# Column sums of squares: a group of four products waits for all four squares

## The chip, the cores and the metric

One Trainium2 chip, one of its cores. The metric is the time of one execution on the device in microseconds; lower is better. Names of engines: PE is TensorE's matmul, PEld its weight load, DVE is VectorE, ACT is ScalarE, POOL is GpSimd, SP is SyncE.

## The reference

A two-layer decoder trunk in float32. 512 prompt tokens and 8 x 4 sample tokens, 544 columns in all, of 1024 channels. Layer 0 mixes tokens by causal pooling, layer 1 by a gated linear recurrence (HGRN2); each is followed by a gated ConvFFN. Every sub-layer has a norm ahead of it and one behind it:

```python
def rmsnorm(x, g):
    xf = x.astype(jnp.float32)
    r = lax.rsqrt(jnp.mean(xf * xf, axis=-1, keepdims=True) + EPS)
    return (xf * r * g.astype(jnp.float32)).astype(x.dtype)

for li in range(DEPTH):
    h = rmsnorm(x, norm_mix_pre[li])
    m = pool_mixer(h, ...) if li % 2 == 0 else hgrn_mixer(h, ...)
    x = x + rmsnorm(m, norm_mix_post[li])
    h = rmsnorm(x, norm_ffn_pre[li])
    m = conv_ffn(h, ...)          # gelu(conv(h @ w_up)) * ..., then @ w_down
    x = x + rmsnorm(m, norm_ffn_post[li])
```

What matters here is the mean of x*x over the 1024 channels, for every token.

## The kernel before

Channels lie on the 128 partitions in eight tiles (k = 0 to 7), tokens along the free dimension, cut into a first half of 256 columns and a second of 288 (256 prompt tokens and the 32 samples). The large products of the layers, which I call ordinary matmuls, run with each operand split into a high and a low part and three matmuls per tile (xh or oh and xl or k are the split activations, wh and wl the split weights; of the names in the lists below, ps and pa are PSUM banks).

A norm's sum over channels is a sum over partitions and over the eight tiles. ScalarE squares each tile (sqs[k], a tile named t). The function colsums then multiplies each square with a 128x32 block of ones (from the tile cs), in full float32 precision, so that 32 partitions of the result hold the sum of that tile. Tile k goes to the partitions 32*(k % 4) to 32*(k % 4) + 31 of one bank named pr; tiles 4 to 7 are added on top of 0 to 3. Four products of one call therefore write four different strips of 32 partitions and use four different strips of 32 columns of the matmul array. Behind them, ScalarE copies the bank out (t<-pr), col_rstd sums the four strips by three small products (pr<-cs,t, 128x1 and 32x1), VectorE works out the reciprocal root in a chain of small operations (tiles named c) and scales a unit matrix by it, and one product with ones (pr<-t,cs 128x256 or 128x288) spreads the factor over all partitions, from where ScalarE copies it to R. Results of a large product leave PSUM by a VectorE multiplication with R.

colsums is called twice (tiles 0 to 3, then 4 to 7) for each half at four norms: in project (the pooled layer's output) and in Residual.start_b (the norm ahead of a ConvFFN or of HGRN2, when the sub-layer before it is added to x). That makes 64 products, 32 of 256 columns and 32 of 288.

The order of the instructions is not that of the code. Every operation is recorded by Plan; Plan.emit is a list scheduler with a cost and a latency per engine, which writes out the order of all five engines. It takes at each step the operation that can start first by its estimates, and of those that can start at the same time one of a pr bank first, then the one with the longest tail behind it. Plan.after(a, b, ...) adds to the next recorded operation a dependency on the last writer of each tile given. In colsums each product has its own square as an input, and Plan.after adds the square of the last tile of the call. ScalarE's squares are scheduled as well, so the square of the last tile is not always the last to be made.

Of the kernel before, what the change touches and what calls it, by code (L numbers as in the profile page):

```python
# [345 lines left out]
def trunk_step(ctx: ExitStack, tc: _tile.TileContext, xT, xp, xs, spool, s0, fctx, par, gb0, cst, bands,  # L346
               pw, wup, wdn, win, wout, yT, yB, o_pp, o_ps, o_hp, o_hs, o_ff):
    nc = tc.nc
    plan = Plan(tc)
# [300 lines left out]
    def colsums(pn, sqs, ks):  # L650

        for k in ks:
            j = k % 4 * 32
            plan.after(sqs[ks[-1]])
            PE.matmul(pn[j:j + 32], ones[:, 0:32], sqs[k], start=(k < 4), stop=(k >= 4), skip_group_check=True)

    def spread(dg, out):
# [74 lines left out]
    class Residual:  # L732
# [10 lines left out]
        def start_b(self, hf):  # L743
# [17 lines left out]
            for k0, k1 in (((0, 2), (2, 4), (4, 6), (6, 8)) if gnext is None else ((0, 1), (1, 2), (2, 4), (4, 6), (6, 8))):  # L761
                mk = m[:, k0:k1, sl]
                if self.gpost is None:
                    DVE.tensor_tensor(mk, mk, rpost.unsqueeze(1).broadcast_to([P, k1 - k0, n]), op=ALU.mult)
                else:
                    for k in range(k0, k1):
                        DVE.scalar_tensor_tensor(m[:, k, sl], m[:, k, sl], pcol(self.gpost + k), rpost, op0=ALU.mult, op1=ALU.mult)
                if gnext is None:

                    POOL.dma_start(yT[:, k0:k1, sl], mk, accum_op=ALU.add)  # L770
                    continue
                xs_ = xs_of(k0, k1, sl)
                DVE.tensor_tensor(xs_, xs_, mk, op=ALU.add)
                for k in range(k0, k1):
                    xk = x_of(k, sl)
                    ACT.activation(oh[:, k, sl], xk, AF.Identity, scale=pcol(gnext + k))
                    sqs[k] = tt((P, n))
                    ACT.activation(sqs[k], xk, AF.Square)
                    if k:
                        low(k - 1)  # L780
                    if k % 4 == 3:
                        colsums(pn, sqs, range(k - 3, k + 1))
# [75 lines left out]
    def project(hf):  # L858
        sl = HV[hf]
        n = sl.stop - sl.start  # L860
        pn = pap.tile([P, 512], F32, tag="pa", name="pr")[:, 0:n]
        sqs = {}
        order = (0, 1, 4, 5, 2, 3, 6, 7)
        for at, o in enumerate(order):
            gi, oc = o // 2, o % 2
            d = ps1()[:, 0:n]
            for kk in range(2):
                s = slice(kk * 256 + oc * P, kk * 256 + (oc + 1) * P)
                PE.matmul(d, pws[gi][:, s], pooled(2 * gi + kk, sl), start=(kk == 0), stop=(kk == 1))
            sq = sqs[at] = tt((P, n))  # L870

            if o % 2:
                DVE.tensor_scalar(mp[:, o, sl], d, pcol(O_PSC + o), None, op0=ALU.mult)
                ACT.activation(sq, mp[:, o, sl], AF.Square)
            else:
                ACT.activation(sq, d, AF.Square, scale=pcol(O_PSC + o))
                ACT.activation(mp[:, o, sl], d, AF.Identity, scale=pcol(O_PSC + o))
            if at % 4 == 3:
                colsums(pn, sqs, range(at - 3, at + 1))
        accp[hf] = tt((P, n))  # L880
        ACT.activation(accp[hf], pn, AF.Identity)
# [910 lines left out]
```

## Time and profile before

| | us |
|---|---|
| median of three runs | 1161.19 |
| lowest and highest | 1158.9, 1162.99 |
| the profiled execution | 1161.18 |
| its span from first to last instruction | 1159.3 |
| TensorE busy in it | 1143.8 |
| VectorE, ScalarE, GpSimd busy | 870.1, 685.8, 406.4 |
| mean granted TensorE clock | 0.995 of full speed |

How to read it: a row of the profile names the line of the code, the engine, the operation, the tile written and the tiles read, the shape and a count; the lines of all recorded operations are that of the scheduler's call (L312), so that tile names tell them apart. A product of float32 stands as two matmul records in the profile and as one row in the lists of instructions here. The halves' column counts, 256 and 288, tell the two halves apart.

### The profile page before, as it was taken

The page shows a single profiled execution, that of the slowest core. Times are in us where ns is not written, and L with a number is a line of the kernel's source. Part 1 is how long each engine was busy: PE and PEld are TensorE (multiplying, and loading weights), DVE is VectorE, ACT ScalarE, POOL GpSimd, SP SyncE. Part 2 cuts the span into 40 slices and gives each one's busy share as a digit, 9 for nine tenths or more (in the row PEclk, how much of TensorE's full clock was granted, in tenths as well). Part 3 has the DMA queues.
Part 4 walks back from the last instruction along what each step waited for, and adds up shares of the span by engine and source line. Part 5 has one row for each costly group of instructions (what it writes and reads, how often), then busy time and mean ns, then how long its engine had stood idle before and what let it go on. Part 6 is the DMA issues. An engine that isn't in the chain of part 4 may idle for free.

```text
span 1159.3 us, 26118 instructions
## 1 busy us (share of the span) xinstructions
PE 1143.8 (99%) x9860; PEld 1104.2 (95%) x9860; DVE 870.1 (75%) x2068; ACT 685.8 (59%) x1459; POOL 406.4 (35%) x729
## 2 busy tenths in 40 slices
PE   8999999999999999999999999999999999999996
PEld 7789999999999998999999999979999999999996
DVE  6679977988788776576766785458986897878865
ACT  4546555656566575566666764455565665656653
POOL 3435222433443332443443420224621434343322
PEclk9999999999999999999999999999999999999999
DMA  9876167676876765777667642573536767777543
GB/s 317 206 189 133 55 175 178 169 179 171 195 172 159 206 208 115 156 149 162 154 157 154 135 127 101 149 188 79 132 83 187 190 167 180 174 169 192 115 127 77
DMA packets 90397, 183.48 MB, mean 158 GB/s; under 512 B 10522, under 2 KB 17050, under 8 KB 90264
## 3 DMA queue, kind: packets, MB, share of 16 engines
q0 software_dynamic: 48272, 91.90, 40.0%
q1 hardware_dynamic: 41856, 89.88, 23.7%
q8 instruction: 77, 1.26, 0.4%
q14 instruction: 48, 0.39, 0.1%
q10 hardware_dynamic: 144, 0.05, 0.0%
HBM read 156.00 MB, written 12.77 MB: 146 GB/s over the span
## 4 chain that ended last, share of the span: by engine, by line
PE 96%; DMA 1%; DVE 1%; ACT 1%; issue 0%; SPq 0%; POOL 0%; DVEq 0%; ACTq 0%; POOLq 0%
PE pa L312 47%; PE ps L312 46%; PE pr L312 3%; DMA t<-bands 1%; DMA wh<-win 0%; DVE t L312 0%; ACT A L312 0%; DVE x L312 0%; ACT t L312 0%; DVE m L312 0%; SPq L312 0%; DVE c L312 0%; ACT wl L312 0%; POOL t L312 0%; DVEq L1772 0%
## 5 line engine op out<-in xcount | busy, mean ns | idle before, releaser
L312 ACT ACTIVATE wh<-raw 128x512 fp32r<-128x512 f32 (+2 forms) x280 | 163.9, 598 | 158.5 <-PE pa L312 59.7
L312 PE MATMUL pa<-op,wh 128*128 128x272 f32 x1152 | 255.7, 288 | 0.0
L312 PE MATMUL ps<-t,wh 128*128 128x272 f32 x1248 | 236.5, 288 | 0.0
L312 DVE TENSOR_TENSOR wl<-raw,wh 128x512 fp32r<-128x512 f32 (+2 forms) x280 | 179.1, 652 | 75.3 <-ACT wh L312 73.2
L312 PE MATMUL pa<-op,wl 128*128 128x272 f32 x768 | 221.2, 288 | 0.0
L312 PEld LDWEIGHTS ps<-t,wh 128*128 128x128 f32 x1248 | 195.9, 188 | 0.0
L312 PEld LDWEIGHTS pa<-op,wh 128*128 128x128 f32 x1152 | 192.9, 188 | 0.0
L312 PE MATMUL ps<-t,wl 128*128 128x272 f32 x624 | 179.5, 288 | 0.0
L312 POOL COPY fst<-t 128x16 f32<-128x16 f32 (+1 forms) x176 | 92.8, 581 | 246.3 <-DVE t L312 246.2
L312 DVE TENSOR_TENSOR t<-t 128x512 f32<-128x512 f32 (+10 forms) x331 | 138.5, 441 | 45.6 <-ACT t L312 23.7
L312 PE MATMUL ps<-xh,wh 128*128 128x256 f32 (+1 forms) x560 | 165.7, 297 | 0.0
L312 PE MATMUL ps<-xl,wh 128*128 128x256 f32 (+1 forms) x560 | 162.3, 290 | 0.0
L312 PE MATMUL ps<-xh,wl 128*128 128x256 f32 (+1 forms) x560 | 161.1, 288 | 0.0
L312 DVE SCALAR_TENSOR_TENSOR t<-t,prm 128x560 f32<-128x560 f32 (+1 forms) x184 | 141.1, 796 | 4.6 <-ACT t L312 3.6
L312 PEld LDWEIGHTS pa<-op,wl 128*128 128x128 f32 x768 | 144.4, 188 | 0.0
L312 PE MATMUL pa<-k,wh 128*128 128x272 f32 (+2 forms) x560 | 137.4, 289 | 0.0
L312 PEld LDWEIGHTS ps<-t,wl 128*128 128x128 f32 x624 | 117.5, 188 | 0.0
L312 ACT ACTIVATE t<-t 128x544 fp32r<-128x544 f32 (+5 forms) x145 | 85.0, 596 | 44.0 <-DVE t L312 42.3
L312 PEld LDWEIGHTS ps<-xh,wh 128*128 128x128 f32 x560 | 105.2, 188 | 3.8 <-issue 0.9
L312 PEld LDWEIGHTS ps<-xl,wh 128*128 128x128 f32 x560 | 105.5, 188 | 2.6 <-issue 2.0
L312 PEld LDWEIGHTS ps<-xh,wl 128*128 128x128 f32 x560 | 105.4, 188 | 2.5 <-issue 2.4
L312 PEld LDWEIGHTS pa<-k,wh 128*128 128x128 f32 x560 | 97.5, 188 | 1.3 <-issue 1.3
(208 smaller groups left out, 2501.9 us busy)
## 6 DMA issues: line engine op xcount, KB each, us to landing
raw<-wup SPq DMA_DIRECT2D x37, 512.0 KB, 3.2
raw<-wup SPq DMA_DIRECT2D x64, 256.0 KB, 3.8
raw<-wup POOLq DMA_DIRECT2D x64, 256.0 KB, 5.8
wh<-win POOLq DMA_DIRECT2D x58, 256.0 KB, 3.4
wl<-win POOLq DMA_DIRECT2D x58, 256.0 KB, 4.7
m<-t POOLq DMA_DIRECT2D x48, 272.0 KB, 6.2
wh<-wup POOLq DMA_DIRECT2D x34, 256.0 KB, 4.2
wl<-wup POOLq DMA_DIRECT2D x34, 256.0 KB, 5.9
```

Source lines behind the costliest of these rows:

```text
L312: o[1](*o[3], **o[4])
```

## The change

In colsums each of the products now depends on the last writers of all the tiles of the call, not on that of the last tile alone:

```diff
         for k in ks:
             j = k % 4 * 32
-            plan.after(sqs[ks[-1]])
+
+            plan.after(*(sqs[q] for q in ks))
             PE.matmul(pn[j:j + 32], ones[:, 0:32], sqs[k], start=(k < 4), stop=(k >= 4), skip_group_check=True)
```

No product, square or copy is added or removed. The scheduler, given the other dependencies, writes out another order. The SP queue's order stays the same; the other four differ in places. Of the sixteen groups of four, six stood together before and do after: four in project, and the two of the first half behind the first ConvFFN, which stand in one row of eight; ten were apart and now stand together.

C, the second half behind the first ConvFFN. PE before (pr_1121 is the bank of the sums, t_1122 to t_1125 are the squares of tiles 0 to 3):

```order
L312 MATMUL ps_1103<-xh_1058,wh_1080 128x256
L312 MATMUL pr_1121<-t_1125,cs_80 32x288
L312 MATMUL ps_1103<-xl_107,wh_1080 128x256
L312 MATMUL ps_1103<-xh_1058,wl_1081 128x256
L312 MATMUL pr_1121<-t_1124,cs_80 32x288
L312 MATMUL ps_1103<-xh_1058,wh_1086 128x256
L312 MATMUL ps_1103<-xl_107,wh_1086 128x256
L312 MATMUL pr_1121<-t_1122,cs_80 32x288
L312 MATMUL ps_1103<-xh_1058,wl_1087 128x256
L312 MATMUL pr_1121<-t_1123,cs_80 32x288
L312 MATMUL ps_1102<-xh_1058,k_1040 128x256
```

Now, at the same place of PE:

```order
L312 MATMUL ps_1102<-xh_1058,k_1044 128x256
L312 MATMUL pr_1121<-t_1122,cs_80 32x288
L312 MATMUL pr_1121<-t_1123,cs_80 32x288
L312 MATMUL pr_1121<-t_1124,cs_80 32x288
L312 MATMUL pr_1121<-t_1125,cs_80 32x288
L312 MATMUL ps_1102<-xl_107,k_1044 128x256
```

The four products have moved together, and the first of them stands nine ordinary matmuls later than the first did. ACT before at C, which makes these squares and those of tiles 4 to 7:

```order
L312 ACTIVATE t_1125<-x_1011 128x288
L312 ACTIVATE t_1124<-x_1011 128x288
L312 ACTIVATE t_1122<-x_1010 128x288
L312 ACTIVATE t_1123<-x_1010 128x288
L312 ACTIVATE xh_1058<-x_1010,prm_79 128x288
L312 ACTIVATE t_1126<-x_1012 128x288
L312 ACTIVATE t_1129<-x_1013 128x288
```

The square of the last tile, t_1125, is the first to be made, and that is the one which each product waited for beside its own. ACT now at the same place:

```order
L312 ACTIVATE t_1124<-x_1011 128x288
L312 ACTIVATE t_1125<-x_1011 128x288
L312 ACTIVATE t_1122<-x_1010 128x288
L312 ACTIVATE t_1123<-x_1010 128x288
L312 ACTIVATE xh_1058<-x_1010,prm_79 128x288
L312 ACTIVATE t_1126<-x_1012 128x288
L312 ACTIVATE t_1127<-x_1012 128x288
```

Four squares ahead of the group, as before, in nearly the same order.

B, the second half of the pooling layer's norm. PE before (pr_250 is the bank, t_251 to t_254 the squares):

```order
L312 MATMUL pr_250<-t_254,cs_80 32x288
L312 MATMUL pa_268<-xh_104,k_200 128x256
L312 MATMUL pa_268<-xl_107,k_200 128x256
L312 MATMUL pr_250<-t_253,cs_80 32x288
L312 MATMUL pa_268<-xh_104,k_202 128x256
L312 MATMUL pa_268<-xh_104,k_200 128x256
L312 MATMUL pr_250<-t_251,cs_80 32x288
```

Now:

```order
L312 MATMUL pa_268<-xh_104,k_202 128x256
L312 MATMUL pa_268<-xh_104,k_200 128x256
L312 MATMUL pr_250<-t_251,cs_80 32x288
L312 MATMUL pr_250<-t_252,cs_80 32x288
L312 MATMUL pr_250<-t_253,cs_80 32x288
L312 MATMUL pr_250<-t_254,cs_80 32x288
L312 MATMUL pa_268<-xl_107,k_200 128x256
```

The group stands one ordinary matmul later than the first product did. ACT at B now, with the copy to xh among the four squares, where before it followed them:

```order
L312 ACTIVATE t_253<-x_101 128x288
L312 ACTIVATE xh_104<-x_101,prm_79 128x288
L312 ACTIVATE t_251<-x_100 128x288
L312 ACTIVATE t_252<-x_100 128x288
L312 ACTIVATE t_254<-x_101 128x288
```

One copy has moved ahead of three of the squares.

A, the first half of the same norm. PE before (pr_190 is the bank, t_192 to t_198 squares; pr_233 is the small sum of another half):

```order
L312 MATMUL pr_190<-t_195,cs_80 32x256
L312 MATMUL pr_190<-t_198,cs_80 32x256
L312 MATMUL pa_268<-xh_104,k_199 128x256
L312 MATMUL pr_190<-t_196,cs_80 32x256
L312 MATMUL pa_268<-xl_107,k_199 128x256
L312 MATMUL pa_268<-xh_104,k_201 128x256
L312 MATMUL pr_233<-cs_80,t_188 128x1
L312 MATMUL pr_190<-t_197,cs_80 32x256
L312 MATMUL pr_233<-cs_80,t_188 128x1
L312 MATMUL pr_233<-cs_80,t_188 32x1
```

Now:

```order
L312 MATMUL pr_190<-t_191,cs_80 32x256
L312 MATMUL pr_190<-t_192,cs_80 32x256
L312 MATMUL pr_190<-t_193,cs_80 32x256
L312 MATMUL pr_190<-t_194,cs_80 32x256
L312 MATMUL pr_233<-cs_80,t_188 128x1 x2
L312 MATMUL pr_233<-cs_80,t_188 32x1
L312 MATMUL pa_268<-xh_104,k_201 128x256
```

One of the two groups stands directly ahead of the small sum, the other five ordinary matmuls behind it.

## Prediction

> **What bounds the kernel now.** I read the shares of the engines first, then the chain that ended last by engine, then the list of what TensorE itself waited for (total us, times, longest).
>
> ```profile
> PE 1143.8 (99%) x9860; PEld 1104.2 (95%) x9860; DVE 870.1 (75%) x2068; ACT 685.8 (59%) x1459; POOL 406.4 (35%) x729
> ...
> PE 96%; DMA 1%; DVE 1%; ACT 1%; issue 0%; SPq 0%; POOL 0%; DVEq 0%; ACTq 0%; POOLq 0%
> ```
>
> ```profile
> PE pr L312 <- ACT t L312: 0.9, 1, 0.9
> ```
>
> TensorE (PE) is busy for 1143.8 of 1159.3 us and holds 96% of the chain. It waited for a square once, 0.9 us. So a microsecond of TensorE's own time saved is a microsecond of the program's, unless a wait that is not there today takes its place. Two questions remain: what a column-sum product costs TensorE alone and beside others, and whether the squares are ready where the new order wants them.
>
> **The price of a block.** I call products that stand with no other matmul between them a block. Around the blocks TensorE starts ordinary matmuls at an even pace; a block is priced by how far it spreads them. Two long pieces of the chain give that pace (start, length, count):
>
> ```profile
> 461.39 19.06 PE pa L312 x144
> ...
> 733.92 11.48 PE pa L312 x96
> ```
>
> The first is all matmuls of 288 columns, 19.06/144 = 0.132 us each; the second all of 256, 11.48/96 = 0.120. Now lone products of 288 columns in TensorE's timeline (start, duration; a product is two records, so x2 is one product and x8 four; durations overlap, so I go by starts):
>
> ```profile
> 448.87 0.28 PE L312 MATMUL ps<-xl,wh 128*128 128x256 f32 x1
> 449.07 0.67 PE L312 MATMUL pr<-t,cs 128*32 128x288 f32 x2
> ...
> 449.99 0.67 PE L312 MATMUL pr<-t,cs 128*32 128x288 f32 x2
> ...
> 450.81 0.28 PE L312 MATMUL ps<-xl,k 128*128 128x256 f32 x1
> ```
>
> From 448.87 to 450.81 are 1.94 us. Three ordinary matmuls start in it (448.87, one after each product), 3 x 0.12 = 0.36; the rest, 1.58, is 0.79 per product. Four products in one block:
>
> ```profile
> 46.67 0.28 PE L312 MATMUL ps<-xh,wh 128*128 128x256 f32 x1
> 46.88 0.69 PE L312 MATMUL pr<-t,cs 128*32 128x288 f32 x8
> 47.51 0.38 PE L312 MATMUL ps<-xl,wh 128*128 128x256 f32 x1
> 47.73 0.28 PE L312 MATMUL ps<-xh,wl 128*128 128x256 f32 x1
> ```
>
> 47.73 - 46.67 - 2 x 0.12 = 0.82 us for all four. So four cost what one costs: the four column strips of the array work at once, and most of the price is paid per block. With 256 columns, lone products and then three in one block:
>
> ```profile
> 752.99 0.30 PE L312 MATMUL pa<-oh,wl 128*128 128x288 f32 x1
> 753.21 0.62 PE L312 MATMUL pr<-t,cs 128*32 128x256 f32 x2
> ...
> 754.88 0.29 PE L312 MATMUL pa<-oh,wl 128*128 128x288 f32 x1
> ...
> 757.56 0.29 PE L312 MATMUL pa<-oh,wl 128*128 128x288 f32 x1
> 757.78 0.63 PE L312 MATMUL pr<-t,cs 128*32 128x256 f32 x6
> 758.35 0.41 PE L312 MATMUL pa<-oh,wh 128*128 128x288 f32 x1
> 758.59 0.29 PE L312 MATMUL pa<-k,wh 128*128 128x288 f32 x1
> ```
>
> Lone (a second one stands in the rows left out, and three ordinary matmuls start): (1.89 - 3 x 0.132)/2 = 0.75. Three: 1.03 - 2 x 0.132 = 0.77; I take 0.77 for four as well, an estimate from these rows.
>
> Row first: three in one block take 0.77 where one takes 0.75, and four 0.82 where one takes 0.79. A rule of the Trainium skill promises less: its page TensorE: Matmul & The Clock Gate (Part 3: Packing small matmuls, the measured speedup) gives 2.38x for three column tiles and 3.07x for four row tiles. An estimate from that page is that four side by side cost 4/3.07 = 1.3 lone ones, and the sum below would be 14.7 instead of 16.6 us. The trace disagrees with it, and I go by the trace.
>
> **The change, part by part.** It removes no product and adds none: 64 before, 64 after. It moves them, and the list of instructions counts the blocks. Five places change, all in the rest of each sub-layer's norm: A, the pooling layer's first half (256 columns), B its second (288), C the second half after the first ConvFFN (288), D and E the two halves after HGRN2 (256, 288). Blocks before and after: A 6 to 2, B 6 to 2, C 7 to 2, D 6 to 2, E 7 to 2.
>
> In A two of the six stand among other full-precision products and cost less, as does one of the two after:
>
> ```profile
> 51.74 0.62 PE L312 MATMUL pr<-t,cs 128*32 128x256 f32 x2
> 52.29 0.54 PE L312 MATMUL pr<-cs,t 128*128 128x1 f32 x4
> ```
>
> 52.29 - 51.74 = 0.55, and I take it for all three. The terms, all of them TensorE's own time on the path:
> - A: 4 x 0.75 + 2 x 0.55 = 4.10 before, 0.55 + 0.77 = 1.32 after: saves 2.78.
> - B: 6 x 0.79 = 4.74, 2 x 0.82 = 1.64: saves 3.10.
> - C: 7 x 0.79 = 5.53, 1.64: saves 3.89.
> - D: 6 x 0.75 = 4.50, 2 x 0.77 = 1.54: saves 2.96.
> - E: like C, 3.89.
>
> Sum 16.6 us. The bounds of the change in TensorE's work are 0 (blocks that cost per product) and 24.4 (all blocks gone); the measured 0.82 puts it near the value taken.
>
> **The wait it adds.** All four products now stand in TensorE's queue behind the last of four squares, and whatever follows stands behind them. The cover is that the scheduler places the group later. In C the squares (ScalarE) and the first product of before are:
>
> ```profile
> 445.99 1.45 ACT L312 ACTIVATE t<-x 128x288 f32<-128x288 f32 x4 [3.22 <-DVE x L312]
> ...
> 447.76 1.43 ACT L312 ACTIVATE t<-x 128x288 f32<-128x288 f32 x4
> ```
>
> ```profile
> 447.00 0.67 PE L312 MATMUL pr<-t,cs 128*32 128x288 f32 x2
> ```
>
> The fourth square ends at 447.44. The group stands nine ordinary matmuls behind the place of the first product, so TensorE gets there at 447.0 + 9 x 0.12 = 448.1: 0.6 later than needed. The second group follows after 0.82 + 11 x 0.12, at 450.2; its squares end at 449.2. D and E come out alike, by 0.4 us or more. B is the tight one:
>
> ```profile
> 64.43 0.67 PE L312 MATMUL pr<-t,cs 128*32 128x288 f32 x2
> ```
>
> ```profile
> 63.34 1.45 ACT L312 ACTIVATE t<-x 128x288 f32<-128x288 f32 x4 [3.77 <-DVE x L312]
> ```
>
> There the group moves by one matmul only, to 64.55, and ScalarE now has one more copy (0.4) among the four squares: the fourth would end at 63.34 + 1.45 + 0.4 = 65.2, 0.6 too late. But the product that spreads the half's norm, which starts this chain, now stands ten ordinary matmuls further ahead of the group (1.2 us), so I charge nothing. If that cover is gone, B loses 0.6.
>
> Nothing else is bought or paid: the eight products after the first ConvFFN's first half already stand in one row and go at the pace of the squares, and the last one is not earlier or later.
>
> ```profile
> 432.47 2.82 PE L312 MATMUL pr<-t,cs 128*32 128x256 f32 x16 [0.86 <-ACT t L312]
> ```
>
> TensorE will wait about 1 us longer ahead of them and finish them at the same moment, the eighth square's. SP's DMA order is unchanged; POOL's and ScalarE's change within a few rows, and neither holds TensorE today. The profiled execution took 1161.18 us beside its span of 1159.3, and the median of the runs is 1161.19, so they are the same: 1161.2 - 16.6 = 1144.6.
>
> **The rivals.**
>
> First, VectorE takes part of it back. Behind A and B comes a stretch in which VectorE is full:
>
> ```profile
> 130.00:140.00 10.00, 10.00 (x82) 10.00 (x81) 10.00 (x21) 6.96 (x14) 5.36 (x8) 1.00 0.01 2
> ```
>
> (the columns: sum of TensorE, weight loads, VectorE, ScalarE, POOL.) If VectorE can't be earlier, A's and B's 5.9 us are lost: 1150.5. Against it: its load starts with the norm's factor, which moves with TensorE, and in that stretch it still caught up and waited for TensorE:
>
> ```profile
> 129.26 0.79 DVE L312 TENSOR_TENSOR t<-ps,R 128x512 f32<-128x512 f32 x2 [0.61 <-PE ps L312]
> ```
>
> Second, TensorE stands at the groups. Where it arrives with one square ready, it waits for three more, about 1.45 - 0.43 = 1.0 us; at nine groups 9: 1153.6. The margins above speak against it.
>
> Third, the other side: the sum is late and TensorE runs out of work. From the last product to the norm's factor R it is 8.0 us in C:
>
> ```profile
> 453.81 0.67 PE L312 MATMUL pr<-t,cs 128*32 128x288 f32 x2
> ```
>
> ```profile
> 461.42 0.41 ACT L312 ACTIVATE R<-pr 128x288 f32<-128x288 f32 x1 [4.37 <-PE pr L312]
> ```
>
> Results of the second half can't leave their PSUM banks before R. If TensorE stood still under this chain in the three second halves (B, C, E), that is 24 us: 1168.6. It decides from 16.6/3 = 5.5 us each. Against it: between the group and the factor's product the new order keeps 40 and more ordinary matmuls, about 5 us, that need no R of this half.
>
> Fourth, the four strips don't work at once at these places as they do at 46.88. If one of the four falls out of step, a group costs two blocks, 1.50 or 1.58 instead of 0.77 or 0.82; over nine groups that is 6.8 us: 1151.4. The one block of four and the one of three above speak against it. By the estimate from the Trainium skill's page TensorE: Matmul & The Clock Gate it would be 1.9 us and 1146.5.
>
> Fifth, the moves do nothing, since something unseen paces the whole program: 1161.2. Only a TensorE that waits somewhere speaks for it, and it doesn't.
>
> **How the numbers follow.** Chances: the sum above 0.79 (its own range 1142 to 1148: B's 0.6, the four at 256 columns, and some 2 us from run to run, as the three of before are 1158.9 to 1163.0); VectorE 0.07; waits at the groups 0.05; idle under the chain 0.03; strips out of step 0.03; nothing 0.03. The range goes from 1141.5 to 1151 and so takes in VectorE's case; the other four, 0.14, are left out. A change of under 0.3%, 3.5 us, can't be told from none here. Faster: 0.79 + 0.07 + 0.05 + 0.03 = 0.94; same 0.03; slower 0.03.
>
> **What would show it.** In the new timeline each of the five places has two blocks of x8, 0.7 us long, among ordinary matmuls. TensorE's wait on a square stays one, now about 2 us, at the eight products; its busy time falls to about 1126 us, and each of the five places is 2.8 to 3.9 us shorter. A second wait of TensorE on ScalarE's squares at B would show the tight margin; waits on VectorE between 80 and 145 us the first rival; a wait of 5 us and more ahead of a second half's evacuation the third. I am wrong if blocks of x8 take 1 us and more, or if TensorE's idle time grows by over 5 us.

## The result and the profile after

| | before | after |
|---|---|---|
| median of six runs each, us | 1160.99 | 1142.42 |
| lowest and highest | 1158.84, 1162.99 | 1141.91, 1146.92 |
| the profiled execution, us | 1161.18 | 1142.5 |
| its span | 1159.3 | 1140.7 |

The ratio is 0.9851, with an interval of 0.9835 to 0.9867: faster by 18.6 us, where 16.6 were predicted. In a later comparison on another occasion (the second run of the changed kernel, below) it was 1143.54 against 1160.0, a ratio of 0.9853 [0.9839, 0.9867], or 16.5 us.

The same two lines of the page, the shares of the engines and the chain by engine, now of the changed kernel:

```profile
PE 1125.2 (99%) x9860; PEld 1097.3 (96%) x9860; DVE 869.8 (76%) x2068; ACT 685.2 (60%) x1459; POOL 408.4 (36%) x729
...
PE 95%; DMA 1%; ACT 1%; DVE 1%; issue 1%; POOL 0%; SPq 0%; DVEq 0%; ACTq 0%; POOLq 0%
```

TensorE is busy for 1125.2 us instead of 1143.8, with the same 9860 matmuls, and still holds the chain. The saving is TensorE's own time. Place C in TensorE's timeline of the changed kernel (start, duration, count):

```profile
440.08 0.69 PE L312 MATMUL pr<-t,cs 128*32 128x288 f32 x8
...
441.87 0.28 PE L312 MATMUL pa<-xh,wl 128*128 128x256 f32 x1
441.99 0.28 PE L312 MATMUL pa<-xh,wh 128*128 128x256 f32 x1
442.20 0.69 PE L312 MATMUL pr<-t,cs 128*32 128x288 f32 x8
442.82 0.38 PE L312 MATMUL pa<-xl,wh 128*128 128x256 f32 x1
443.04 0.28 PE L312 MATMUL pa<-xh,wl 128*128 128x256 f32 x1
```

Two blocks of x8, 0.7 us long, stand where seven blocks stood. By starts, the second costs 443.04 - 441.99 - 2 x 0.12 = 0.81 us. What TensorE waited for, in the list of its waits:

```profile
PE ps L312 <- DVE t L312: 3.2, 1, 3.2
PE pa L312 <- DVE t L312: 1.1, 2, 0.9
PE pa L312 <- DVE wz L312: 1.0, 1, 1.0
PE pr L312 <- ACT t L312: 0.9, 1, 0.9
```

One wait on a square, 0.9 us, the same as before, where I had said about 2. It is the row of eight:

```profile
424.05 2.59 ACT L312 ACTIVATE t<-x 128x256 f32<-128x256 f32 x8 [1.20 <-DVE x L312]
424.52 2.79 PE L312 MATMUL pr<-t,cs 128*32 128x256 f32 x16 [0.85 <-ACT t L312]
```

The first line holds the eight squares, 0.32 us each. The first product starts 0.47 us behind the start of the first square; the fourth is made only at about 425.3.

**Where the time came from.** Both traces hold the same 9860 matmul records, and far from the five places in the same order, so the record with the same number, counted from the start, can be looked up in both. The table compares the changed kernel with the third trace of the kernel before (taken as an experiment; its clock behaves like that of the changed kernel's trace, see below). Each row names the start of one record ahead of or behind a place (behind A and B the two orders still differ a little, so that there the number of matmuls done is the same and not always the matmul):

| place | before, us | after, us | ahead by | of this, the place | predicted |
|---|---|---|---|---|---|
| ahead of A | 40.22 | 40.21 | 0.01 | | |
| behind A | 62.00 | 59.10 | 2.90 | 2.9 | 2.78 |
| behind B | 85.17 | 79.08 | 6.09 | 3.2 | 3.10 |
| ahead of C | 444.14 | 436.04 | 8.10 | | |
| behind C | 457.09 | 445.01 | 12.08 | 4.0 | 3.89 |
| ahead of D | 711.25 | 700.09 | 11.16 | | |
| behind D | 759.50 | 745.28 | 14.22 | 3.1 | 2.96 |
| behind E | 788.09 | 770.03 | 18.06 | 3.8 | 3.89 |

The five places give 17.0 us for 22 blocks fewer (32 before, 10 after), 0.77 a block. Between the places the two drift by 2.0 and -0.9 us, of which one wait of 1.2 us at 193 us of the older kernel, on VectorE, is the largest part. Behind E nothing is given back: the last row stands 18.06 ahead, and at 1118.01 it is 18.4.

**The two microseconds too many.** In my first trace of the kernel before the granted TensorE clock was low at 32 to 36 us. Windows of the first trace of before (the columns: sum of TensorE, weight loads, VectorE, ScalarE, POOL, then the clock, DMA share, GB/s):

```profile
32.00:34.00 2.00, 2.00 (x11) 2.00 (x11) 1.76 (x5) 0.49 (x2) 0.38 (x3) 0.53 1.12 362
34.00:36.00 2.00, 2.00 (x11) 1.89 (x10) 0.40 (x2) 1.46 (x4) 0.00 (x0) 0.61 1.14 297
```

The same windows of the changed kernel:

```profile
32.00:34.00 2.00, 2.00 (x18) 1.96 (x18) 1.96 (x5) 1.05 (x3) 1.03 (x3) 1.00 1.14 355
34.00:36.00 2.00, 2.00 (x11) 1.58 (x11) 1.77 (x5) 1.70 (x5) 0.00 (x0) 1.00 1.13 299
```

In the first of these windows TensorE starts 11 matmuls at half the clock and 18 at the full one, but not the same ones. One stretch of the same 16 matmuls, in the first trace of before and then in the changed kernel:

```profile
31.93 3.63 PE L312 MATMUL ps<-t,k 128*128 128x128 f32 x16
```

```profile
32.14 2.05 PE L312 MATMUL ps<-t,k 128*128 128x128 f32 x16
```

They take 3.63 us instead of 2.05. Summed over windows of half a microsecond, 1 minus the clock gives the time lost, 1.71 us here. Two further traces of the kernel before (runs 9 and 10) don't have this dip, so the old order doesn't always bring it: span 1159.3 - 1140.7 = 18.6, less 1.7, is 16.9. Against those two traces, the time lost to a low clock taken off on both sides, it is 17.6 and 18.1 (table below). The medians can't be split in this way, since the other executions have no trace.

### The profile page after: what moved, and what is told of

It is laid out like the page before. It is cut to its first block, busy times and chain, and to the rows that moved or that the text cites. A ratio compares the mean times of both kernels' runs of the same rounds, so it can differ in the third digit from the quotient of the medians.

```text
span 1140.7 us, 26123 instructions
## 1 busy us (share of the span) xinstructions
PE 1125.2 (99%) x9860; PEld 1097.3 (96%) x9860; DVE 869.8 (76%) x2068; ACT 685.2 (60%) x1459; POOL 408.4 (36%) x729
## 4 chain that ended last, share of the span: by engine, by line
PE 95%; DMA 1%; ACT 1%; DVE 1%; issue 1%; POOL 0%; SPq 0%; DVEq 0%; ACTq 0%; POOLq 0%
PE pa L312 47%; PE ps L312 46%; PE pr L312 2%; DMA wh<-win 1%; DMA k<-xp 1%; ACT A L312 0%; DVE t L312 0%; ACT t L312 0%; DVE x L312 0%; ACT wl L312 0%; DVE m L312 0%; POOL t L312 0%; DVE c L312 0%; SPq L312 0%; ACT q L312 0%
## 5 line engine op out<-in xcount | busy, mean ns | idle before, releaser
L312 ACT ACTIVATE t<-t 128x544 fp32r<-128x544 f32 (+5 forms) x145 | 85.0, 596 | 45.9 <-DVE t L312 44.3
```

The source lines that it names most:

```text
L312: o[1](*o[3], **o[4])
```

## The experiments

All are compared with the kernel before, measured on the same occasion. Prices of a block are worked out as in the prediction. The strips are the four groups of 32 columns. The diffs show the main lines, with ... for the others; the remarks behind # are mine.

**1. The products alone moved.** Before's dependency and before's order of everything else (but for 12 more small filler matmuls, pa<-wz, which Plan.emit lays into the gaps of the order that it is given); at the very end, the products of each group of four are moved on TensorE to the place of the last of them:

```diff
+        plan.groups.append([len(plan.ops) - 1 - q for q in range(len(ks))])   # colsums, behind its loop
...
+        at = {i: t for t, i in order}                                         # Plan.emit, ahead of the writing out
+        last = {i: max(at[q] for q in g) for g in self.groups for i in g}
+        order = [(last.get(i, t), i) for t, i in order]
```

> The order of before on all engines, with one edit: the products of each group of four are moved down to the place of their last one on TensorE. Theory of blocks (a block of column-sum products costs TensorE about 0.8 us whether it holds one or four): all of the gain, 16.6 us, 1144.4 at a median of 1161.0 before. Rival (the gain comes from the other order of ScalarE, VectorE and POOL that the scheduler wrote): within 0.3% of before, 1161. If the rest of the measured 18.6 us is the TensorE clock at the start of an execution and not the change, the sum of the five places in the two timelines is 16.6 here as well.

Measured 1145.14 against 1160.65 of before, ratio 0.986 [0.9841, 0.9879]. The grouping on TensorE carries most of the gain; what the scheduler does on the other engines after the change is not its source. The blocks stand at the same price:

```profile
441.35 0.28 PE L316 MATMUL ps<-xh,wl 128*128 128x256 f32 x1
441.55 0.69 PE L316 MATMUL pr<-t,cs 128*32 128x288 f32 x8
442.18 0.39 PE L316 MATMUL ps<-xh,k 128*128 128x256 f32 x1
442.40 0.28 PE L316 MATMUL ps<-xl,k 128*128 128x256 f32 x1
```

442.40 - 441.35 - 2 x 0.12 = 0.81. Looked up as in the table, with the fillers left out, A and B together give 6.2 us against the third trace of before, C 4.0, D 3.0 and E 3.9: 17.1, as in the changed kernel. Its span, 1143.7, is still 3.0 us longer than the changed kernel's. Of this 1.1 stands already at 27 us, ahead of A, where the fillers lie, and most of the rest grows between the places, in part by waits of TensorE of 0.3 to 0.6 us; what brings these isn't shown. Its TensorE is busy for 1127.1 us, against 1125.2 of the changed kernel.

**2. Each product with its own square only.** The line with plan.after is taken out:

```diff
-            plan.after(sqs[ks[-1]])
             PE.matmul(pn[j:j + 32], ones[:, 0:32], sqs[k], ...)
```

> Each product waits for its own square alone. By the list of instructions the blocks are 7 in A, 8 each in B, C, D and E (32 before, 10 after in these five), and 7 each in the two halves of the pooling layer's projection, where they were 2 and where neighbours are full-precision products (0.55 us a block). Theory of blocks: against the changed kernel B, C, E +4.7 us each, D +4.5, A +3.9, the projection up to 2 x 2.75: 1165 to 1170, slower than before by 4 to 9. Rival (TensorE's time does not go with the number of blocks): between the changed kernel and before.

Measured 1176.55, ratio 1.0131 [1.0112, 1.015]: slower, as expected, but by more. A lone product at C:

```profile
459.06 0.28 PE L312 MATMUL ps<-xh,wh 128*128 128x256 f32 x1
459.27 0.67 PE L312 MATMUL pr<-t,cs 128*32 128x288 f32 x2
459.87 0.39 PE L312 MATMUL ps<-xl,wh 128*128 128x256 f32 x1
460.10 0.28 PE L312 MATMUL ps<-xh,wl 128*128 128x256 f32 x1
```

460.10 - 459.06 - 2 x 0.12 = 0.80. The blocks go from 32 to 39 at the five places and from 4 to 14 in project, 17 more. The trace's span is 1175.1, 16.3 above that of the third trace of before; a low clock from 34.7 to 41.5 us lost 3.4 of it, and the 12.9 left are 0.76 for each of the 17 blocks. The price that I took too low is that of project's blocks, 0.55:

```profile
45.48 0.67 PE L312 MATMUL pr<-t,cs 128*32 128x288 f32 x2
46.09 0.75 PE L312 MATMUL pa<-pooled,t 128*128 128x288 f32 x2
46.77 0.67 PE L312 MATMUL pr<-t,cs 128*32 128x288 f32 x2
```

The two pooled records between the products start 0.243 us apart where nothing stands between them; 46.77 - 45.48 - 2 x 0.243 = 0.80. The 0.55 had been measured beside products of a single column.

**3. Full-width products.** 128 columns of ones instead of 32, all eight tiles added in one place, grouped as in the changed kernel (col_rstd divides by 128 copies instead of 32):

```diff
-            PE.matmul(pn[j:j + 32], ones[:, 0:32], sqs[k], start=(k < 4), stop=(k >= 4), ...)
+            PE.matmul(pn, ones, sqs[k], start=(k == 0), stop=(k == KT - 1), ...)
```

> The changed kernel with products of full width, 128 columns of ones, that accumulate all eight tiles on all 128 partitions (the later division by the number of copies is 128 instead of 32). They stay in groups of four by the list of instructions (eight in A). The strips work at once in the changed kernel: then full-width products cost 0.49 us for the first of a block (the row of the product that spreads R) and 0.24 (288 columns) or 0.21 (256) for each further one, 1.21 and 1.08 for four against 0.82 and 0.77: B, C, E +0.8 each, D and A +0.6 each, the projection +1.2, 1147 (1145 to 1149). If the strips do not work at once: no slower than the changed kernel, 1142 or less.

Measured 1161.36, ratio 1.0008 [0.9996, 1.002]. The forecast failed. Four in a block:

```profile
451.04 0.28 PE L312 MATMUL ps<-xh,wl 128*128 128x256 f32 x1
451.16 2.10 PE L312 MATMUL pr<-t,cs 128*128 128x288 f32 x8
452.88 0.49 PE L312 MATMUL ps<-xh,k 128*128 128x256 f32 x1
453.21 0.28 PE L312 MATMUL ps<-xl,k 128*128 128x256 f32 x1
```

453.21 - 451.04 - 2 x 0.12 = 1.93: four times 0.48, and a full-width product alone costs 0.48 or 0.49 too, in every trace. So a full-width product has no price per block, and four of them share nothing. Over 14 groups (eight of 288 columns, 1.93 for 0.82; six of 256, 1.73 for 0.77) that is 14.6 us more than the changed kernel. The spans differ by 19.6 (1160.3 and 1140.7). Of the other 5.0 a low clock from 37.2 to 40.6 us lost 1.7, two waits on squares at 29 and 31 us took 1.3, and 2.0 were not traced. So what four strips share is the time of one product on the array; full-width products gain nothing by standing together.

**4. Groups of eight.** One call of colsums for each half, in the residual norms (shown) and in project (the same edit, with `at` for `k`):

```diff
-                    if k % 4 == 3:
-                        colsums(pn, sqs, range(k - 3, k + 1))
+                    if k == KT - 1:
+                        colsums(pn, sqs, range(KT))
```

> One group of eight for each half instead of two groups of four, waiting for all eight squares; in the list of instructions all eight stand in one block everywhere. Theory of blocks: the second round of four costs 0.24 (288 columns) or 0.21 (256) inside a block instead of a block of its own: 0.58, 0.56 saved per half in A to E, 2.8 us, and up to 0.7 in the projection: 1139 to 1140. Rival: the sums come later, since the first four are not taken early, and TensorE waits ahead of the norm's factor: 1142 or more.

Measured 1145.27, ratio 0.9867 [0.9852, 0.9883]; not better than groups of four. The blocks did become cheaper; at C:

```profile
444.73 0.28 PE L312 MATMUL pa<-xl,wh 128*128 128x256 f32 x1
444.93 1.18 PE L312 MATMUL pr<-t,cs 128*32 128x288 f32 x16
446.04 0.39 PE L312 MATMUL pa<-xh,wl 128*128 128x256 f32 x1
446.27 0.28 PE L312 MATMUL pa<-xh,wh 128*128 128x256 f32 x1
```

446.27 - 444.73 - 2 x 0.12 = 1.30 for eight, against 1.64 for two blocks of four. At B the block was dearer:

```profile
69.31 1.94 PE L312 MATMUL pr<-t,cs 128*32 128x288 f32 x16
70.08 0.44 ACT L312 ACTIVATE t<-x 128x288 f32<-128x288 f32 x1 [5.09 <-PE pr L312]
70.58 0.14 PEld L312 LDWEIGHTS pr<-t,cs 128*32 128x32 f32 x2 [0.63 <-ACT t L312]
```

ScalarE makes one of the eight squares only at 70.08; seven products go ahead, and the eighth's weights are loaded at 70.58, when its square is done. This block costs 2.07 us. So the cheaper blocks should give 6 x 0.34 - 0.43 = 1.6 us (the row of eight left out). TensorE also stood still for 0.67 us at 29.3 and 0.43 at 44.3, and the clock was low from 27 to 35 us, which lost 3.4 us; without this its span would be 0.9 us shorter than that of the changed kernel.

**5. The changed kernel once more**, nothing edited.

> The changed kernel once more, for the spread of its times and a second trace. Blocks theory: 16.6 to 17.0 us below the kernel before where both kernels' TensorE runs at the full clock from 15 us on. The trace of before had the granted clock at 0.5 from 32.2 to 35.8 us (about 1.7 us of work lost), that of the changed kernel had not. If this dip comes and goes from one execution to the next, whatever the order, it will stand in this trace or in some of the times (1142.4 without it, about 1144 with one, 1146 with a double one). If the new order removes it, none of these times lies above 1143.5.

Measured 1143.54 (1141.87 to 1143.87), ratio 0.9853 [0.9839, 0.9867]. Its trace has the span of the first, 1140.7, and no low clock at 30 to 40 us. Three of its five times lie above 1143.5, by 0.04 to 0.4 us; none comes near the 1146 of a double dip. Its blocks cost the same. What set the other four executions apart isn't shown, as they have no trace.

**6 and 7. Two strips instead of four.** The order of all instructions is that of the changed kernel; only the strips of the sums change, 0, 1, 0, 1 in run 6 and 0, 0, 1, 1 in run 7 (2 and 3 for the second group):

```diff
-            j = k % 4 * 32
+            j = (k % 2 + k // 4 * 2) * 32      # run 6, with start=(k % 4 < 2)
+            j = k // 2 * 32                    # run 7, with start=(k % 2 == 0)
```

> The changed kernel with the order of every instruction kept; only the strips differ: the four products of a group go to strips 0, 1, 0, 1 (second group 2, 3, 2, 3) instead of 0, 1, 2, 3. Theory that the four strips work at once, and that a block costs about 0.3 us for going in and out plus 0.48 (288 columns) or 0.43 (256) for each round of products that share a strip: the groups have two rounds, 1.30 and 1.20 us instead of 0.82 and 0.77, as the blocks of eight had; over 14 groups (the row of eight after the first ConvFFN goes at the pace of its squares) 8 x 0.48 + 6 x 0.43 = 6.4 us: 1148.8. Rival, a price per block whatever stands in it up to four: 0.82 and 0.77 again, 1142.4.

> As the run before, but the strips go 0, 0, 1, 1 (second group 2, 2, 3, 3). Theory that the strips work at once, but products are started strictly in order, so that the second of a strip holds back the first of the next: three rounds, 0.3 + 3 x 0.48 = 1.77 us at 288 columns and 0.3 + 3 x 0.43 = 1.63 at 256; over 14 groups 8 x 0.95 + 6 x 0.86 = 12.8 us: 1155.2. If a waiting product lets the next one past, two rounds as in the run before: 1148.8. Rival, a price per block: 1142.4.

Measured 1148.21, ratio 0.9896 [0.9883, 0.991], and 1148.07, ratio 0.9894 [0.988, 0.9908]. The second group at C, in run 6 and then in run 7:

```profile
445.79 0.28 PE L312 MATMUL pa<-xh,wh 128*128 128x256 f32 x1
446.00 1.17 PE L312 MATMUL pr<-t,cs 128*32 128x288 f32 x8
447.09 0.39 PE L312 MATMUL pa<-xl,wh 128*128 128x256 f32 x1
447.32 0.28 PE L312 MATMUL pa<-xh,wl 128*128 128x256 f32 x1
```

```profile
446.05 0.28 PE L312 MATMUL pa<-xh,wh 128*128 128x256 f32 x1
446.26 1.17 PE L312 MATMUL pr<-t,cs 128*32 128x288 f32 x8
447.36 0.39 PE L312 MATMUL pa<-xl,wh 128*128 128x256 f32 x1
447.58 0.28 PE L312 MATMUL pa<-xh,wl 128*128 128x256 f32 x1
```

Both cost 1.29 us where four strips cost 0.81, and the spans are 1146.7 and 1146.3 against 1140.7: 6.0 and 5.6 us for 6.4 expected. This is the experiment that settles the mechanism: the same instructions in the same order, and the price follows the number of products that share a strip. A price per block alone falls. The single records, two for each product, say the same: at the second group of C, four records start within 0.02 us at 442.20 in the changed kernel and four more at 442.47, while in run 7 there are two at a time, at 446.26, 446.53, 446.77 and 447.01. Run 7 takes two rounds as well, so the second product of a strip does not hold back the first of the next strip. A strip of columns and the partitions of the bank that it writes go together in all these runs, so which of the two makes the second product wait is not told apart; run 3's price, 0.48 for a full-width product alone as well as for each of four, fits the array.

**8. Groups of eight in the residual norms only**; project keeps its fours (the second half of run 4's edit is left out).

> Groups of eight in the norms of the residual sums alone; project keeps its groups of four. Blocks theory: at A, B, C, D, E one block of eight (1.30 or 1.20 us) for two of four (1.64 or 1.54): 0.34 x 5 = 1.7 us below the changed kernel, 1140.7; this holds if the clock dip of the run with groups of eight everywhere (0.5 from 27.1 to 34.3 us) came from project's part of the order. Rival, the eight products come so late that the factor R is late and TensorE waits: 1142.4 or more, with new waits of TensorE on VectorE or PSUM behind B, C or E.

Measured 1146.51 (1144.98 to 1148.76), ratio 0.9883 [0.9867, 0.99]. The rival held: the blocks cost 1.20 to 1.31, and the time did not fall; in the profiled execution (the longest of the four) TensorE had a new wait of 2.0 us ahead of a matmul whose operand VectorE was late with:

```profile
135.48 0.41 PE L312 MATMUL ps<-t,wh 128*128 128x272 f32 x2
137.90 0.59 PE L312 MATMUL ps<-t,wh 128*128 128x272 f32 x1 [2.01 <-DVE t L312]
```

That is the end of the stretch in which VectorE is full (22.9 of 24 us from 110 to 134 us). The wait was paid for twice, since from 137.4 us, within it, the clock was low; the window that follows it:

```profile
138.00:140.00 2.00, 2.00 (x9) 2.00 (x10) 2.00 (x6) 0.65 (x1) 0.00 (x0) 0.50 0.02 4
```

Nine matmuls in 2 us; the dip ended at about 141 and lost 1.7 us. The dip at the start of this execution was also twice as long as in the changed kernel's traces, 1.7 us more. How much of the wait belongs to the order is open: the factor R of B is copied at 77.7 us here, at 76.1 in run 4, whose A and B have groups of eight too, and at 69.3 in the changed kernel, and run 4 waits at that place for 0.15 us only. So groups of four are the best version here: no run was faster than the changed kernel.

**9 to 11. The clock.** The kernel before twice more and groups of eight once more, one execution each (1158.66, 1160.78 and 1147.86 us; one more of before, without a trace, took 1162.59).

> The kernel before once more, for the granted clock behind 15 us. Its first trace had the clock at 0.5 from 32.2 to 35.8 us. If that dip comes from chance, it may be absent here, and the span is then about 1157.5 instead of 1159.3; if it comes from before's order, it stands here too, at the same place.

> The kernel before a third time, for the same question: a dip behind 15 us that is there in one trace and not in the next belongs to chance, and the span follows it by half its length.

> Groups of eight everywhere once more. Its first trace had the clock at 0.5 from 27.1 to 34.7 us, and all its four times lay within 1 us. If the dip comes from this order (TensorE stands for 0.7 us at 29.3), it is here again and the time is 1145; if it is chance, the time without it is 1141 to 1142.

The time that TensorE lost by a low clock, from the windows (one stretch until 19 us, one later):

| trace | span, us | lost until 19 us | lost later | span less lost |
|---|---|---|---|---|
| before, first | 1159.3 | 1.7 | 1.7 (32 to 36) | 1155.9 |
| before, second | 1156.6 | 0 | 0 | 1156.6 |
| before, third | 1158.8 | 1.7 | 0 | 1157.1 |
| after, first | 1140.7 | 1.7 | 0 | 1139.0 |
| after, second | 1140.7 | 1.7 | 0 | 1139.0 |
| eights, first | 1143.2 | 1.7 | 3.4 (27 to 35) | 1138.1 |
| eights, second | 1146.1 | 3.4 | 3.4 (31 to 38) | 1139.3 |
| run 1 | 1143.7 | 1.7 | 0 | 1142.0 |
| run 2 | 1175.1 | 1.7 | 3.4 (34 to 42) | 1170.0 |
| run 3 | 1160.3 | 1.7 | 1.7 (37 to 41) | 1156.9 |
| run 6 | 1146.7 | 1.7 | 0 | 1145.0 |
| run 7 | 1146.3 | 1.7 | 0 | 1144.6 |
| run 8 | 1146.6 | 3.4 | 1.7 (137 to 141) | 1141.5 |

The window of 32 to 34 us in the second trace of before, at the full clock:

```profile
32.00:34.00 2.00, 2.00 (x17) 1.84 (x16) 1.73 (x6) 1.44 (x4) 0.40 (x3) 1.00 1.13 363
```

For before the later dip comes by chance: in one trace of three. With groups of eight it stood in both traces, twice as long, and run 2 has one as long; two traces suggest that the order of run 4 is prone to it and don't show it. Between 45 us and TensorE's last matmul the only dip in any trace is that of run 8 at its wait. What sets one off at 27 to 37 us was not settled.

## Why the prediction was right, point by point

- **The price of a block: right.** 0.81 or 0.82 and 0.76 or 0.77 us at nine of the ten groups; the tenth stands among other full-precision products. The term that I had only estimated, four products of 256 columns at 0.77 from a block of three, measured 0.77 at D.
- **The five terms: right** within 0.15 us each, 17.0 together for 16.6. In A one of the two blocks that I priced at 0.55 stands between the pooled products and costs 0.75 (44.06 - 42.82 - 2 x 0.243 in the trace of before), which is 0.2 us of the rest.
- **The wait that the change adds: wrong in mechanism.** "All four products now stand in TensorE's queue behind the last of four squares" does not happen. Plan.after binds the scheduler's order; on the chip a product waits for its own square. The row of eight shows it: it starts at 424.52 with 0.85 of idle, behind the first square, and goes at the pace of the squares, as it did before (0.86). Run 4's block at B shows it again: seven of eight products done, one waiting for its square. So the margins that I counted at C, D and E, and B's 0.6 us, were bounds on a wait that would only have stretched a block. At B both blocks cost 0.82 and TensorE waits for nothing.
- **The rest: not forecast.** The medians give 18.6 us in the first comparison and 16.5 in the second, for 16.6 forecast; the traces, without the time lost to a low clock, 16.9 to 18.1. Beside the 17.0 of the five places stands a drift between them, 2.0 and -0.9 us in the traces compared, which no term of the sum held. I also subtracted from one execution without asking whether its clock was usual: it held a dip of 1.7 us that two other traces of the kernel lack. The medians of before, 1160.99, 1160.65 and 1160.0, lie 0.2 to 1.2 us under the 1161.2 that I took, so the base was off by no more than that. That one comparison came within 0.1 us of the forecast is luck.
- **VectorE takes it back: no.** After B the changed kernel was 7.5 us ahead of the first trace of before at 80 us, and still 7.5 at 145 (6.1 of it from A and B, most of the rest the dip). In run 8, which makes the sums later, the wait of 2.0 us came in that very stretch, in its one trace; run 4, with sums nearly as late, has 0.15 there. So VectorE can take time back at this place, and how near the changed kernel is to it isn't shown.
- **Late sums, strips out of step: no.** No wait ahead of a second half's evacuation, and no group at twice the price. The estimate from the Trainium skill's page TensorE: Matmul & The Clock Gate (Part 3, measured speedup: 3.07x for four row tiles) is not what these runs show for four column strips: four lone products at 0.80 against one block at 0.82 are 3.9x.

What I had run together is now apart. A product of 288 columns takes 0.48 us of array time whatever its width (full-width alone 0.48, each further round of strips 0.48), and a block in strips between ordinary matmuls costs 0.32 beside (0.80 - 0.48). Four in one block share both; eight share the 0.32 alone.

## What to carry to other kernels

Small products that write different strips belong side by side with nothing between them: here one such block costs what one lone product costs, and each block that is saved is worth 0.75 to 0.8 us of TensorE. Grouping pays less where a strip is used twice: each further round costs 0.48 us, and only the 0.32 is saved. A larger group also makes its result later, and an engine that is already full may not make that up. Before a forecast is made from one trace, look at the granted clock window by window: here the time lost to its dips is 0 in one trace of the kernel before and 3.4 us in another.

## What the runs showed of the hardware beyond that

- Every dip of the granted clock ahead of TensorE's last matmul lasts 3.41 or 6.83 us at 0.5 of full speed, and so loses 1.71 us or twice that. The Trainium skill's page TensorE: Matmul & The Clock Gate (Part 1, What's actually happening) states a window of 3413 ns and two states, half and full, and the traces agree. It puts the half clock down to an idle window; the dip at 32 us of before does not show that, since TensorE's records fill that window (2.00 of 2.00 us) and no gap of over 0.1 us stands in the 20 us ahead of it. The records leave open how busy the array is within them: from 28.8 to 31.0 us stand 18 matmul records of 32 columns each.
- A full-precision product of 32 columns costs more alone (0.80 us) than one of 128 columns (0.48). The difference of 0.32 us is paid once for a block, however many products stand in it: 0.82 for four and 1.30 for eight. Beside products of one column it is less: a lone product of 256 columns cost 0.55 there, where a full-width one costs 0.43 (run 3, 1.73 for four).
